# GLU output tiles in the score-row buffers, own buffers for the second half of w_out, and feed-forward products written ahead of the last tile's transposes

## The chip, the cores and the metric

One core of a Trainium2 chip runs one inference step of a hybrid encoder layer. The metric is the device time of one execution in microseconds (us).

## What is computed

The layer takes 2048 prompt frames and 64 sample frames of width 1024. All matrix products are in float32 accuracy: each operand is split into a high and a low part, and three products (high by high, high by low, low by high) are summed. Cut to what matters here:

```
hm   = rmsnorm(x) * (1 + scale) + shift
proj = hm @ w_in                      # q, k, v of 8 heads, forget logits, u of the S5 groups
att  = softmax(q k^T / 8 + F_t - F_s) @ v, causal     # F: running sum of log sigmoid(gate)
z    = gelu(S5 scan of u)
ssm  = z * sigmoid(z @ w_glu)                         # the GLU
mix  = concat(att, ssm)
x    = x + g1 * rmsnorm(mix @ w_out)
hf   = rmsnorm(x) * (1 + scale2) + shift2
f    = (silu(hf @ w_gate) * (hf @ w_up)) @ w_down
x    = x + g2 * rmsnorm(f)
```

## The kernel before, in words

The stages follow one another: input projections and S5 scan (to about 696 us), the GLU and then attention head by head (to about 1275 us), the output projection tile by tile (to about 1480 us), the gate and up products of the feed-forward layer (to about 2407 us), and the down product. The text of the program says what depends on what; the framework then sets the order of the instructions on each engine by a schedule of its own, so that a piece that is written early may stand late and the reverse. Every engine takes its own instructions strictly in that order. Loads and stores are issued by the queues of SP (nearly all) and ACT (the GLU's outputs) and by POOL. The transfers of SP and ACT share eight completion counters, dealt out in turn in one common order: an issue that takes a counter waits until the transfer eight places ahead in that order has landed.

**GLU** (`glu`, L914 to L958). `ZS` holds z in DRAM. For each of 4 column blocks b, four tiles `zr` (or `row1` buffers, for odd b) are loaded from `ZS`, split into `zh` and `zl`, and for each of 4 output row blocks o two halves are computed: 12 products into a PSUM bank (L945 to L947), a tanh on ACT (L949) into the tile `mo`, and a product with z on DVE (L953). When both halves of a tile are done, ACT issues its store to `MIXS` (L951), behind the first tanh of the next tile. `mo` is one of two buffers named "raw"; these two also serve the cached keys and values of the sample heads (L1086) and the second half of w_out (L1197).

**Attention** (`scores` L982, `values` L1043). For each head h and each block qb of 512 frames, SP loads `qs`, `kk`, `fb` and `vv` (L994 to L998). The scores of 128 frames fill one row buffer: four `row0` buffers for even qb, four `row1` buffers for odd. ACT takes the exponential (L1029). `values` transposes the rows on PE (L122), ACT copies them out of PSUM (`ph`, `pf`: L1067, L1064), and PE multiplies by `vv` (L1071, L1072). The GLU's end and the loads of head 0 overlap.

**Second half of w_out** (`wo_half`, L964). Four pieces of 128 by 1024 are loaded into "raw" (L970); ACT copies each into its high part `woh` (L974), POOL subtracts into the low part `wol` (L975). A "raw" buffer is free again when POOL is done.

**mix0** (`mix_half`, L1164) prepares the first tile of the output projection from `MIXS`: a load, a scaling on POOL (L1172), a subtraction on DVE (L1179), into buffers `mr`, `mh`, `ml` of its own.

**Turn to the feed-forward layer** (L1382 to L1408). Tile t=16 (the 64 sample rows) is the last of the output projection. Its two sums in PSUM go through two norms (L1263 to L1280), the transposes to `hf` (L122), a store to `HB`, and combinations `bh`, `bl` of column blocks (L1321). The gate and up products are formed from seven combinations of blocks (index i) for two matrices; L1449 is the matmul. The first three weight tiles are split ahead of time (`pre`). `weight_sums` forms the combinations of weights on POOL at tile 12.

Of the kernel before, what the change touches and what calls it, by code (L numbers as in the profile page):

```python
# [9 lines left out]
F32 = mybir.dt.float32  # L10
# [9 lines left out]
D = 1024  # L20
KD = 8
NP = 2048
# [46 lines left out]
def hybrid_layer(ctx: ExitStack, tc: tile.TileContext, I, O):  # L69
# [844 lines left out]
    def glu():  # L914
        def load(b, j):
            if b % 2 == 0:
                z = gw.tile([128, L, GC], F32, name="zr", bufs=4)
            else:
                z = at.tile([128, NP], F32, name="row1", bufs=4)[:, :L * GC].rearrange("p (s c) -> p s c", s=L)
            sp.dma_start(z, ZS[j * 128:(j + 1) * 128, :, b * GC:(b + 1) * GC])  # L920
            return z

        nb = CH // GC
        zr = [[load(0, j) for j in range(4)], [load(1, j) for j in range(4)]]
        out = None
        for b in range(nb):
            zz = []
            for hf in range(2):
                for j in range(4):
                    zh = gw.tile([128, 4, GC], F32R, name="zh", bufs=8)  # L930
                    zl = gw.tile([128, 4, GC], F32R, name="zl", bufs=8)
                    split(zh, zl, zr[b][j][:, 4 * hf:4 * hf + 4])
                    zz.append((zh, zl))
            if b + 2 < nb:
                zr.append([])
            for o in range(4):
                os_ = slice(o * 128, (o + 1) * 128)
                mo = raws[-1].tile([128, 2, 512], F32, name="raw", bufs=2)
                mo = mo.rearrange("p a b -> p (a b)")[:, :L * GC]
                mv = mo.rearrange("p (c s) -> p s c", s=L)  # L940
                for hf in range(2):
                    ps = bank("pt")[:, :4 * GC]
                    for k in range(4):
                        zh, zl = zz[4 * hf + k]
                        pe.matmul(ps, glu_h[:, k, os_], zh, start=k == 0, stop=False)  # L945
                        pe.matmul(ps, glu_h[:, k, os_], zl, start=False, stop=False)
                        pe.matmul(ps, glu_l[:, k, os_], zh, start=False, stop=k == 3)  # L947
                    s = slice(4 * hf, 4 * hf + 4)
                    act.activation(mv[:, s], ps.rearrange("p (s c) -> p s c", c=GC), AF.Tanh, scale=0.25)  # L949
                    if hf == 0 and out is not None:  # L950
                        act.dma_start(*out)  # L951
                        out = None
                    dve.scalar_tensor_tensor(mv[:, s], mv[:, s], 1.0, zr[b][o][:, s], op0=OP.add, op1=OP.mult)  # L953
                    yield
                out = (MIXS[os_, b * L * GC:(b + 1) * L * GC], mo)
                if b + 2 < nb:
                    zr[b + 2].append(load(b + 2, o))
        act.dma_start(*out)  # L958
# [4 lines left out]
    def wo_half(pool_, half, raw_of, lo_eng):  # L963
        h_ = pool_.tile([128, 4, D], F32R, name=f"woh{half}")  # L964
        l_ = pool_.tile([128, 4, D], F32R, name=f"wol{half}")
        for k in range(4):
            wo[4 * half + k] = h_[:, k], l_[:, k]
        for k in range(4):
            raw = raw_of()
            sp.dma_start(raw, w_out[:, 4 * half + k, :])  # L970
            if half:
                yield
                yield
            act.activation(h_[:, k], raw, AF.Copy)  # L974
            lo_eng.tensor_sub(l_[:, k], raw, f32(h_[:, k]))  # L975
            yield
# [184 lines left out]
        for _ in xs:  # L1161
            pass

    def mix_half(mp, t, half, bufs):  # L1164
        r = 128 if t < 16 else 64
        b, q = (t // 4, t % 4 * 128) if t < 16 else (3, 512)
        src = MIX[b][:, q:q + r] if half == 0 else MIXS[:, t * 128:t * 128 + r]
        s = 0.25 if half else 1.0
        mr = mp.tile([128, 4, 128], F32, name="mr", bufs=min(bufs, MR))
        sp.dma_start(mr[:, :, :r], src.rearrange("(k p) t -> p k t", p=128))  # L1170
        th_ = mp.tile([128, 4, 128], F32R, name="mh", bufs=bufs)
        pool.tensor_scalar(th_[:, :, :r], mr[:, :, :r], s, 0.0, op0=OP.mult, op1=OP.add)  # L1172
        if t == 16:
            tl_ = None
            dst = th_[:, :, 64:128]
        else:
            tl_ = mp.tile([128, 4, 128], F32R, name="ml", bufs=bufs)
            dst = tl_
        dve.scalar_tensor_tensor(dst, mr[:, :, :r], s, f32(th_[:, :, :r]), op0=OP.mult, op1=OP.subtract)  # L1179
        return th_, tl_  # L1180
# [6 lines left out]
    for h in range(H):  # L1187
        st = {"k": [], "v": [], "f": [], "l": {}}
        if h == 1:
            gl_.close()  # L1190
            wop = ctx.enter_context(ExitStack())
            wop2 = wop.enter_context(tc.tile_pool(name="wout2", bufs=1, side="right", reuse_waits="tile"))
        if h:
            side.append(sample_head(h - 1))
        if h == 2:
            side.append(wo_half(wop2, 1, lambda: raws[-1].tile([128, 2, 512], F32, name="raw", bufs=2).rearrange(
                "p a b -> p (a b)"), pool))  # L1197
        if h == H - 1:
            side.append(sample_head(h))
        for qb in range(4):  # L1200
            rows = []
            interleave(scores(h, qb, st, rows), pend, 4 * (qb + 1), n_pend)
            pend, n_pend = values(h, qb, st, rows), 4 * qb + 4
    mix0 = mix_half(wop2, OT[0], 1, 1)
    for g in (*side, pend):
        for _ in g:
            pass
# [122 lines left out]
        return raws_  # L1330

    def weight_sums(fp, raws_):
        src = []
        for m, raw in enumerate(raws_):
            ss = g8_tile()
            s = ss.rearrange("p (i k f) -> p i k f", i=4, k=4)
            x11, x12 = raw[:, 0:4, 0:128], raw[:, 4:8, 0:128]
            x21, x22 = raw[:, 0:4, 128:256], raw[:, 4:8, 128:256]
            sums4(pool, x11, x12, x21, x22, [s[:, i] for i in range(4)])
            pool.dma_start(WST[m][fp].rearrange("p i k -> p (i k)"), ss)  # L1340
            src.append((x11, s[:, 1], x12, s[:, 2], s[:, 0], x22, s[:, 3]))
        return src

    def down_sums(j):
        raw = g8_tile().rearrange("p (a n) -> p a n", a=2)
# [37 lines left out]
    for i, t in enumerate(OT):  # L1383
        if i + 1 < len(OT):
            t2 = OT[i + 1]
            if i >= 2:
                parts[t2, 1] = mix_half(mp, t2, 1, 3)
            parts[t2, 0] = mix_half(mp, t2, 0, 3)
        if i >= 3:
            accs[t] = [bank("mm") for _ in range(2)]  # L1390
            out_half(t, 1, parts.pop((t, 1)), accs[t])
        out_half(t, 0, parts.pop((t, 0)), accs[t])
        if late:
            out_turn(*late)
            combine_for(late[0])
        if i in (9, 11):
            prep(0, (i - 9) // 2, dve, g8)
        if i == 12:
            raws_ = raw_weights(g8, 0)
            src_w = weight_sums(0, raws_)  # L1400
        if i == len(OT) - 1:
            for n_ in range(3):
                pre.append(rsplit(wring[0], [128, 4, 128], src_w[n_ % 2][n_ // 2], ("wh", "wl")))
        late = t, out_norm(t, accs.pop(t))
    out_turn(*late)
    combine_for(late[0])
    p3.close()
# [18 lines left out]
    def ffn_pair(u, fp, after, src_w):  # L1426
# [7 lines left out]
        for i, role in enumerate("ababcbc"):  # L1434
            bh, bl = (b[:, :, :n] for b in blk[i])
            for m in range(2):
                if pre:
                    wh, wl = pre.pop(0)
                else:
                    turn_w[0] += 1  # L1440
                    v = src_w[m][i] if u == 0 else weight(i, m, fp)
                    wh, wl = rsplit(wring[turn_w[0] % 2], [128, 4, 128], v, ("wh", "wl"))
                first = (role, m) not in banks
                if first:
                    banks[role, m] = bank("up")[:, :n]
                acc = banks[role, m]
                for k in range(4):
                    for q, (w, x) in enumerate(((wh, bh), (wh, bl), (wl, bh))):
                        pe.matmul(acc, w[:, k, :], x[:, k], start=first and k == 0 and q == 0,  # L1449
                                  stop=k == 3 and q == 2, skip_group_check=True)  # L1450
# [40 lines left out]
    for u in range(3):  # L1491
        for fp in range(NF // 2):
# [17 lines left out]
            def after(i):  # L1510
                if nxt:
                    prep(nxt, i, (dve, pool)[i % 2], g8)
                if u == 0 and i == 2 and fp + 1 < NF // 2:
                    nxt_w.extend(weight_sums(fp + 1, raws_))
                if u == 0 and i == 5 and fp + 2 < NF // 2:
                    raws_[:] = raw_weights(g8b, fp + 2)

# [144 lines left out]
```

## Time and profile before

| | us |
|---|---|
| three runs | 2883.9 median (2878.4 to 2885.53) |
| the profiled execution | 2882.82 |
| its span in the trace | 2881.0 |
| PE busy | 2658.4 (92%) |
| DVE busy | 2011.6 (70%) |
| ACT busy | 1410.5 (49%) |
| POOL busy | 1309.0 (45%) |

The mean granted TensorE clock of the profiled execution was 0.959 of full speed. The span is the time from the first to the last instruction of the trace; 1.8 us of the execution lie around it. Busy shares are means over all stages. In the strip of 40 slices of 72 us PE stands at 8 or 9 tenths nearly everywhere behind the first quarter; slices 10 to 13 (from 648 us) read 9, 6, 9 and 7, which are the GLU's stretch and that of the second half of w_out, and slice 21, which holds the turn to the feed-forward layer (about 1480 us), reads 7.

### The profile page before, as it was taken

What the parts mean: (1) busy time and instruction counts of PE and PEld (TensorE: products, weight loads), DVE (VectorE), ACT (ScalarE), POOL (GpSimd) and SP (SyncE); (2) the same over time, 40 slices, a digit from 0 to 9 for tenths busy, and PEclk for the clock granted to TensorE, in tenths of its full rate; (3) what the DMA queues carried; (4) which work ended last, traced back from release to release, by engine and by line L of the source; (5) the groups of instructions that cost most, each with busy time, mean ns of one, the idle gap of its engine ahead of it and who ended that gap; (6) DMA issues with size and microseconds to landing.
All of it is one profiled execution on the core that took longest, in us unless ns stands there. A gap on an engine that the chain in (4) does not pass through costs nothing.

```text
span 2881.0 us, 43890 instructions
## 1 busy us (share of the span) xinstructions
PE 2658.4 (92%) x14580; PEld 2297.8 (80%) x14580; DVE 2011.6 (70%) x3591; ACT 1410.5 (49%) x2724; POOL 1309.0 (45%) x1643
## 2 busy tenths in 40 slices
PE   6699988889697999999978999999999999999997
PEld 2478866667575887778768999999998999888775
DVE  4966567654385887755659988996689886567556
ACT  2343454543276887855553333434354544444333
POOL 3673789892144444433527876663247432001002
PEclk8899989989798999999989999999999999999999
DMA  8565766768644344227855554895569777668554
GB/s 249 162 206 113 175 171 173 193 173 230 157 111 107 101 123 125 78 89 228 268 175 197 204 196 186 301 312 173 177 200 322 236 220 239 195 189 300 172 167 154
DMA packets 470499, 543.48 MB, mean 189 GB/s; under 512 B 112560, under 2 KB 322192, under 8 KB 467456
## 3 DMA queue, kind: packets, MB, share of 16 engines
q1 hardware_dynamic: 445616, 454.72, 54.4%
q0 software_dynamic: 22352, 81.63, 7.6%
q10 hardware_dynamic: 2304, 4.33, 0.4%
q8 instruction: 115, 1.88, 0.3%
q14 instruction: 112, 0.92, 0.1%
HBM read 369.29 MB, written 167.07 MB: 186 GB/s over the span
## 4 chain that ended last, share of the span: by engine, by line
PE 65%; POOL 10%; DVE 9%; DMA 7%; issue 5%; ACT 3%; SPq 1%; DVEq 0%; ACTq 0%; POOLq 0%
PE bank L1449 26%; PE bank L122 5%; PE bank L1578 4%; PE bank L1579 4%; PE bank L1577 4%; PE bank L438 4%; PE bank L1072 2%; PE bank L1071 2%; PE bank L1242 2%; PE bank L1243 2%; PE bank L1017 2%; PE bank L1245 2%; PE bank L1018 2%; DVE wl L1368 2%; POOL cm L703 1%
## 5 line engine op out<-in xcount | busy, mean ns | idle before, releaser
L1449 PE MATMUL bank<-bh,wh 128*128 128x384 f32 (+1 forms) x1848 | 597.5, 324 | 23.7 <-DVE u L1462 7.7
L1449 PE MATMUL bank<-bh,wl 128*128 128x384 f32 (+1 forms) x1848 | 595.4, 322 | 0.0
L1449 PE MATMUL bank<-bl,wh 128*128 128x384 f32 (+1 forms) x1848 | 595.3, 322 | 0.0
L1449 PEld LDWEIGHTS bank<-bh,wh 128*128 128x128 f32 x1848 | 349.2, 189 | 29.7 <-issue 13.5
L1449 PEld LDWEIGHTS bank<-bl,wh 128*128 128x128 f32 x1848 | 349.0, 189 | 0.0
L1449 PEld LDWEIGHTS bank<-bh,wl 128*128 128x128 f32 x1848 | 348.9, 189 | 0.0
L1367 ACT ACTIVATE wh<-wv 128x512 fp32r<-128x512 f32 x308 | 193.7, 632 | 268.6 <-PE bank L1449 211.8
L1368 DVE TENSOR_TENSOR wl<-wv,wh 128x512 fp32r<-128x512 f32 x308 | 286.5, 934 | 46.4 <-ACT wh L1367 40.3
L1485 POOL DMA_DIRECT2D HS<-hx x231 | 126.7, 550 | 275.4 <-DVE hx L1478 269.7
L144 POOL TENSOR_SCALAR var<-ss 128x1 f32<-128x1 f32 (+2 forms) x69 | 28.5, 414 | 481.1 <-ACT sq L1615 220.3
L1578 PE MATMUL bank<-wl,hh 128*128 128x512 f32 x608 | 236.3, 390 | 0.0
L1577 PE MATMUL bank<-wh,hh 128*128 128x512 f32 x608 | 235.5, 389 | 0.0
L1579 PE MATMUL bank<-wh,hl 128*128 128x512 f32 x608 | 235.5, 390 | 0.0
L122 PE MATMUL bank<-ident,row 128*128 128x128 f32 (+1 forms) x1120 | 174.9, 275 | 25.6 <-ACT pf L1064 18.4
L1029 ACT ACTIVATE row<-row,mx 128x1024 f32<-128x1024 f32 (+2 forms) x192 | 171.6, 899 | 37.1 <-DMA kk<-KHL 19.0
L1368 DVE TENSOR_TENSOR wl<-g,wh 128x512 fp32r<-128x512 f32 x154 | 171.2, 1119 | 21.7 <-ACT wh L1367 21.4
L122 PEld LDWEIGHTS bank<-ident,row 128*128 128x128 f32 (+1 forms) x1120 | 134.0, 142 | 56.1 <-ACT pf L1064 22.2
L1564 DVE TENSOR_TENSOR wl<-wr,wh 128x512 fp32r<-128x512 f32 x152 | 105.9, 696 | 93.7 <-ACT wh L1563 93.5
L1563 ACT ACTIVATE wh<-wr 128x512 fp32r<-128x512 f32 x152 | 95.0, 625 | 134.7 <-PE bank L1581 117.2
L1570 DVE TENSOR_TENSOR hl<-hr,hh 128x512 fp32r<-128x512 f32 x152 | 105.6, 695 | 74.9 <-ACT hh L1569 74.9
L1367 ACT ACTIVATE wh<-g 128x512 fp32r<-128x512 f32 x154 | 94.6, 629 | 127.7 <-PE bank L1449 100.1
L1022 DVE CUSTOM_DVE_ANT_0 row<-bank,fb,mx 128x512 f32<-128x512 f32 (+2 forms) x192 | 124.0, 646 | 37.0 <-PE bank L1018 23.8
(449 smaller groups left out, 7020.5 us busy)
## 6 DMA issues: line engine op xcount, KB each, us to landing
wv<-WST SPq DMA_DIRECT2D x176, 256.0 KB
HS<-hx POOLq DMA_DIRECT2D x154, 192.0 KB, 4.5
raw<-in_w_in SPq DMA_DIRECT2D x52, 512.0 KB
raw<-in_w_ada SPq DMA_DIRECT2D x48, 512.0 KB
WST<-g POOLq DMA_DIRECT2D x22, 1024.0 KB, 4.4
wr<-WDT SPq DMA_DIRECT2D x88, 256.0 KB
hr<-HS SPq DMA_DIRECT2D x77, 272.0 KB
hr<-HS SPq DMA_DIRECT2D x75, 256.0 KB
```

The costliest lines, as they stand in the source:

```text
L122: pe.transpose(out, in_, ident[:n, :n])
L438: pe.matmul(acc, w[:, k, :], x[k][:, c0:c0 + cn], start=k == 0 and q == 0, stop=k == KD - 1 and q == len(terms) - 1)
L1022: dve.tensor_tensor_reduce(out=row[:, c0:c0 + cn], in0=ps[:, :cn], in1=st["f"][c0 // 1024][:, c0 % 1024:c0 % 1024 + cn], scale=1.0, scalar ...
L1029: act.activation(row[:, c0:c0 + cn], row[:, c0:c0 + cn], AF.Exp, scale=-1.0, bias=mx, accum_out=l4[:, c0 // 1024, i:i + 1])
L1367: act.activation(hi, src, AF.Copy)
L1368: dve.tensor_sub(lo, src, f32(hi))
L1449: pe.matmul(acc, w[:, k, :], x[:, k], start=first and k == 0 and q == 0, stop=k == 3 and q == 2, skip_group_check=True)
L1485: pool.dma_start(HS[i][fp, :, c0:c0 + n], v)
L1564: dve.tensor_sub(wl, wr, f32(wh))
L1577: pe.matmul(acc, hh[:, s], wh, start=st, stop=False)
L1578: pe.matmul(acc, hh[:, s], wl, start=False, stop=False)
L1579: pe.matmul(acc, hl[:, s], wh, start=False, stop=en)
```

## The change

It has three parts. In the GLU the tiles `mo` of the first three column blocks and the first three row blocks take one of the four `row0` buffers; o = 3 and the last column block stay with "raw". The second half of w_out gets two buffers `wr` of its own, and mix0 uses the same two buffers after it, for its load and for its two results. At the feed-forward turn four weight tiles are split ahead, not three; the 48 matmuls that use them are written ahead of t=16's transposes, with a new order of PSUM banks; and the eight weight sums are spread over tiles 13 and 14 in the program's text.

```diff
@@ glu
-                mo = raws[-1].tile([128, 2, 512], F32, name="raw", bufs=2)
-                mo = mo.rearrange("p a b -> p (a b)")[:, :L * GC]
+                if b < nb - 1 and o < 3:
+                    mo = at.tile([128, NP - 512], F32, name="row0", bufs=4)[:, :L * GC]
+                else:
+                    mo = raws[-1].tile([128, 2, 512], F32, name="raw", bufs=2)
+                    mo = mo.rearrange("p a b -> p (a b)")[:, :L * GC]
...
         if h == 2:
-            side.append(wo_half(wop2, 1, lambda: raws[-1].tile([128, 2, 512], F32, name="raw", bufs=2).rearrange(
-                "p a b -> p (a b)"), pool))
+            side.append(wo_half(wop2, 1, lambda: wop2.tile([128, D], F32, name="wr", bufs=2), pool))
...
-    mix0 = mix_half(wop2, OT[0], 1, 1)
+    m_in = wop2.tile([128, D], F32, name="wr", bufs=2)
+    m_hl = wop2.tile([128, 2, 4, 128], F32R, name="wr", bufs=2)
+    mix0 = mix_half(None, OT[0], 1, 1, m_in[:, :512].rearrange("p (k t) -> p k t", k=4), m_hl[:, 0], m_hl[:, 1])
...
         if i == 12:
             raws_ = raw_weights(g8, 0)
-            src_w = weight_sums(0, raws_)
+            src_w, sgen = weight_sums(0, raws_)
+        if i in (13, 14):
+            next(sgen, None)
         if i == len(OT) - 1:
-            for n_ in range(3):
+            for n_ in range(4):
                 pre.append(rsplit(wring[0], [128, 4, 128], src_w[n_ % 2][n_ // 2], ("wh", "wl")))
         late = t, out_norm(t, accs.pop(t))
+    plan.update(up=(4, 5, 0, 1, 2, 3, 6, 7))
+    pre_acc = []
+    for n_, (wh, wl) in enumerate(pre):
+        bh, bl = blk[n_ // 2]
+        acc = bank("up")[:, :384]
+        pre_acc.append(acc)
+        for k in range(4):
+            for q, (w, x) in enumerate(((wh, bh), (wh, bl), (wl, bh))):
+                pe.matmul(acc, w[:, k, :], x[:, k], start=k == 0 and q == 0, stop=k == 3 and q == 2,
+                          skip_group_check=True)
     out_turn(*late)
     combine_for(late[0])
```

The order of the instructions changes at three places. The rows below are in the order in which the engine takes them; a name left of an arrow is written, one right of it read, and brackets name whom the instruction waits for (DMAHW0 to DMAHW7 are the eight shared completion counters).

ACT in the GLU, from the fifth output tile on, before (L949 is the tanh, L951 the store, L1029 the exponential of head 0's first scores):

```order
L949 ACTIVATE raw<-bank_6939 128x4x66 [waits DMAHW1_49,PE_49]
L949 ACTIVATE raw<-bank_6955 128x4x66 [waits PE_49]
L951 DMA MIXS<-raw 128x528 [waits DMAHW1_49,DVE_49]
L1029 ACTIVATE row_7244,l_7243<-row_7244,mx 128x128 [waits DVE_49]
L1029 ACTIVATE row_7301,l_7243<-row_7301,mx 128x256 [waits DVE_49]
L1029 ACTIVATE row_7324,l_7243<-row_7324,mx 128x384 [waits DVE_49]
L949 ACTIVATE raw<-bank_6973 128x4x66 [waits DMAHW6_49]
L949 ACTIVATE raw<-bank_6989 128x4x66 [waits PE_49]
L1029 ACTIVATE row_7349,l_7243<-row_7349,mx 128x512 [waits DVE_49]
L951 DMA MIXS<-raw 128x528 [waits DMAHW4_49,DVE_49]
L949 ACTIVATE raw<-bank_7007 128x4x66 [waits DMAHW1_49,PE_49]
```

The same tiles after (L952 is the tanh, L954 the store):

```order
L952 ACTIVATE row_6938<-bank_6939 128x4x66 [waits PE_49]
L952 ACTIVATE row_6972<-bank_6973 128x4x66 [waits DMAHW4_49,PE_49]
L952 ACTIVATE row_6938<-bank_6955 128x4x66 [waits PE_49]
L952 ACTIVATE row_6972<-bank_6989 128x4x66 [waits PE_49]
L952 ACTIVATE row_7006<-bank_7007 128x4x66 [waits DMAHW6_49,PE_49]
L954 DMA MIXS<-row_6938 128x528 [waits DMAHW4_49,DVE_49]
L954 DMA MIXS<-row_6972 128x528 [waits DMAHW6_49,DVE_49]
L952 ACTIVATE raw<-bank_7041 128x4x66 [waits PE_49]
L952 ACTIVATE row_7006<-bank_7023 128x4x66 [waits PE_49]
```

Up to three tiles are now in work at a time, and the exponentials of head 0 have gone behind the twelfth store of the GLU. The stores still wait for counters.

SP and the second half of w_out: before, the four loads stand among the loads of heads 2 and 3, far behind the GLU; after, they stand right behind the GLU's last tiles, among the loads of the sample heads and of heads 0 and 1. SP after (L973 is the w_out load):

```order
L973 DMA wr<-in_w_out 128x1024 [waits DMAHW5_49,DVE_49,PE_49]
L973 DMA wr<-in_w_out 128x1024 [waits DMAHW6_49]
L1092 DMA raw<-in_cache_k 128x4x64 [waits DMAHW4_49,DMAHW7_49,DMAHW2_49,DVE_49]
L1093 DMA raw<-in_cache_k 128x4x64 [waits DMAHW1_49]
L997 DMA qs<-QHL_60 128x1x512 [waits PE_49]
L1095 DMA raw<-in_cache_v 128x4x64 [waits DMAHW3_49]
L1092 DMA raw<-in_cache_k 128x4x64 [waits DMAHW0_49,DVE_49]
L1093 DMA raw<-in_cache_k 128x4x64 [waits DMAHW5_49]
L1095 DMA raw<-in_cache_v 128x4x64 [waits DMAHW6_49]
L973 DMA wr<-in_w_out 128x1024 [waits DMAHW7_49,Pool_49]
L973 DMA wr<-in_w_out 128x1024 [waits Pool_49]
L997 DMA qs<-QHL_60 128x1x512 [waits DMAHW1_49,PE_49]
```

The first pair waits for the GLU's last reads, the second for POOL to be done with the first; mix0's load stands right behind the last row, and the loads for head 1 behind that.

ACT's copies `woh` after (L977), now in head 0's first two blocks of values:

```order
L1032 ACTIVATE row_7486,l_7398<-row_7486,mx 128x896 [waits DVE_49,Pool_49]
L1055 ACTIVATE rb<-bank_7515 64x512 [waits PE_49]
L1070 ACTIVATE ph<-bank_7521 128x256 [waits PE_49]
L977 ACTIVATE woh_9339<-wr 128x1024 [waits DMAHW5_49,DMASW0_49]
L1070 ACTIVATE z3h<-bank_7538 128x128 [waits PE_49]
L1032 ACTIVATE row_7509,l_7398<-row_7509,mx 128x1024 [waits DVE_49,Pool_49]
L977 ACTIVATE woh_9339<-wr 128x1024 [waits DMAHW6_49]
```

The third and fourth `woh` follow 10 and 14 rows behind the second. Each waits at its place for its load, with the exponentials and copies of head 0 behind it.

PE at the turn to the feed-forward layer, before: the 48 first products stand ahead of t=16's transposes already. The last of them, the transposes (L122, 128x64) and the next products:

```order
L1449 MATMUL bank_16215<-bh_14138,wh 128x384
L1449 MATMUL bank_16215<-bl_14139,wh 128x384
L1449 MATMUL bank_16215<-bh_14138,wl 128x384
L122 MATMUL bank_16082<-ident,xt 128x64 [waits DVE_49,Activation_49]
L122 MATMUL bank_16082<-ident,xt 128x64 x3
L122 MATMUL bank_16091<-ident,xt 128x64 [waits Activation_49]
L122 MATMUL bank_16091<-ident,xt 128x64 x3
L1449 MATMUL bank_16166<-bh_16132,wh 128x384 [waits Activation_49]
```

After, where the first 24 of them (L1426) end and the other 24 begin, around the transposes of the tile before t=16 (128x128):

```order
L122 MATMUL bank_16004<-ident,xt 128x128 [waits DVE_49,Activation_49]
L122 MATMUL bank_16004<-ident,xt 128x128 x3
L122 MATMUL bank_16013<-ident,xt 128x128 [waits Activation_49]
L122 MATMUL bank_16013<-ident,xt 128x128 x3
L1426 MATMUL bank_16123<-bl_14138,wh 128x384
L1426 MATMUL bank_16123<-bh_14137,wl 128x384
L1426 MATMUL bank_16084<-bh_14135,wh 128x384 [waits DVE_49,PE_49]
L1426 MATMUL bank_16084<-bl_14136,wh 128x384
```

Ahead of the same transposes stand the same 48 products, but the last 24 of them now use the banks of t=16's own sums and wait until DVE has read those. The order of the weight sums on POOL at tiles 12 to 14 is what it was.

## Rows read from the trace of the kernel before

**Rows 1.** The page: the chain that ended last, by engine.

```profile
PE 65%; POOL 10%; DVE 9%; DMA 7%; issue 5%; ACT 3%; SPq 1%; DVEq 0%; ACTq 0%; POOLq 0%
```

**Rows 2.** PE's waits, 696 to 775 us: us in total, times, longest.

```profile
PE bank L945 <- ACT raw L949: 30.4, 5, 12.2
```

**Rows 3.** ACT's waits, 696 to 775 us.

```profile
ACT raw L949 <- DMA fb<-FP: 28.7, 3, 10.8
ACT row L1029 <- DMA kk<-KHL: 19.0, 1, 19.0
ACT raw L949 <- DMA MIXS<-raw: 8.1, 3, 4.7
```

**Rows 4.** The chain of work, 700 to 775 us: start, duration, what.

```profile
754.64 11.12 DMA fb<-FP
765.84 0.33 ACTq L951
```

**Rows 5.** Windows: length, busy (instructions) by engine, PEclk, DMA share, GB/s.

```profile
710.00:770.00 60.00, 28.17 (x146) 25.29 (x147) 14.11 (x32) 8.07 (x19) 6.53 (x13) 0.71 0.75 178
...
740.00:750.00 10.00, 3.71 (x17) 3.72 (x18) 2.57 (x6) 3.15 (x10) 2.10 (x4) 0.50 0.97 230
750.00:760.00 10.00, 4.87 (x22) 4.59 (x22) 3.65 (x7) 1.12 (x2) 2.16 (x5) 0.67 1.00 206
```

**Rows 6.** Transfers, 696 to 775 us.

```profile
DMA packets 21182, 14.13 MB, mean 179 GB/s; under 512 B 13498, under 2 KB 16890, under 8 KB 21178
```

**Rows 7.** PE's waits, 855 to 930 us, then ACT's, 780 to 930 us.

```profile
PE bank L122 <- ACT pf L1064: 18.4, 3, 14.4
...
ACT woh L974 <- DMA raw<-in_w_out: 21.8, 3, 14.6
```

**Rows 8.** The chain of work, 855 to 930 us.

```profile
857.19 6.44 DMA raw<-in_w_out
...
868.41 8.62 DMA raw<-in_w_out
...
902.83 12.07 DMA raw<-in_w_out
```

**Rows 9.** Windows of 10 us behind the fourth load of w_out.

```profile
900.00:910.00 10.00, 3.14 (x20) 2.42 (x18) 0.64 (x2) 0.30 (x1) 2.04 (x3) 0.77 0.53 135
910.00:920.00 10.00, 2.51 (x12) 2.51 (x13) 1.89 (x3) 3.01 (x5) 3.92 (x3) 0.50 0.09 30
920.00:930.00 10.00, 10.00 (x58) 8.50 (x56) 6.92 (x21) 6.60 (x14) 4.47 (x6) 0.88 0.29 78
```

**Rows 10.** L974 and L975: duration ns min/median/max, first and last start.

```profile
L974 ACT ACTIVATE woh<-raw x4: 1052/1057/1066, 863.7 to 914.9; 128x1024 fp32r<-128x1024 f32 x4
...
L975 POOL TENSOR_TENSOR wol<-raw,woh x4: 2356/2376/2404, 864.9 to 916.1; 128x1024 fp32r<-128x1024 f32 x4
```

**Rows 11.** ACT's groups, 795 to 830 us: busy, mean ns, idle before.

```profile
L1029 ACT ACTIVATE row<-row,mx 128x1024 f32<-128x1024 f32 (+7 forms) x19 | 18.5, 983 | 4.9 <-DVE mx L1022 3.8 <-issue 1.1
L1067 ACT ACTIVATE ph<-bank 128x512 fp32r<-128x512 f32 (+2 forms) x15 | 7.5, 534 | 1.7 <-PE bank L122 1.7
```

**Rows 12.** The window of head 0's values, 795 to 830 us.

```profile
795.00:830.00 35.00, 34.97 (x213) 27.91 (x212) 31.08 (x93) 29.16 (x65) 13.17 (x14) 1.00 0.30 76
```

**Rows 13.** PE's timeline at the turn; in brackets the idle time before.

```profile
1495.11 1.09 PE L122 MATMUL bank<-ident,xt 64*128 64x64 f32 x8 [12.10 <-DVE xt L1280]
1501.17 1.01 PE L1449 MATMUL bank<-bh,wh 128*128 128x384 f32 x2 [4.98 <-ACT bh L1321]
```

**Rows 14.** L1449's first form, and DVE's reads of t=16's sums.

```profile
L1449 PE MATMUL bank<-bh,wh x1848: 290/334/686, 1473.6 to 2407.3; 128*128 128x384 f32 x124, 128*128 128x288 f32 x61
...
L1264 DVE TENSOR_TENSOR o<-bank,lo x2: 674/678/682, 1484.9 to 1486.9; 64x512 f32<-64x512 f32 x2
```

**Rows 15.** Windows: the first products behind the turn; the step to the down product.

```profile
1500.00:1510.00 10.00, 8.46 (x35) 7.96 (x36) 6.33 (x6) 6.05 (x6) 4.28 (x2) 0.69 0.65 150
...
2400.00:2410.00 10.00, 10.00 (x71) 9.59 (x70) 6.65 (x14) 4.10 (x9) 2.17 (x3) 1.00 0.99 342
```

More of the change, by code (lines that the diff above doesn't have):

```diff
@@ L1162, in interleave, with mix_half @@
             pass
-    def mix_half(mp, t, half, bufs):
+    def mix_half(mp, t, half, bufs, mr=None, th_=None, tl_=None):
         r = 128 if t < 16 else 64
@@ L1168, in mix_half @@
         s = 0.25 if half else 1.0
-        mr = mp.tile([128, 4, 128], F32, name="mr", bufs=min(bufs, MR))
+        if mp:
+            mr = mp.tile([128, 4, 128], F32, name="mr", bufs=min(bufs, MR))
+            th_ = mp.tile([128, 4, 128], F32R, name="mh", bufs=bufs)
         sp.dma_start(mr[:, :, :r], src.rearrange("(k p) t -> p k t", p=128))
-        th_ = mp.tile([128, 4, 128], F32R, name="mh", bufs=bufs)
         pool.tensor_scalar(th_[:, :, :r], mr[:, :, :r], s, 0.0, op0=OP.mult, op1=OP.add)
@@ L1176, in mix_half @@
         else:
-            tl_ = mp.tile([128, 4, 128], F32R, name="ml", bufs=bufs)
+            tl_ = tl_ if mp is None else mp.tile([128, 4, 128], F32R, name="ml", bufs=bufs)
             dst = tl_
@@ L1332, in weight_sums @@
     def weight_sums(fp, raws_):
-        src = []
+        src, work = [], []
         for m, raw in enumerate(raws_):
@@ L1338, in weight_sums, with run @@
             x21, x22 = raw[:, 0:4, 128:256], raw[:, 4:8, 128:256]
-            sums4(pool, x11, x12, x21, x22, [s[:, i] for i in range(4)])
-            pool.dma_start(WST[m][fp].rearrange("p i k -> p (i k)"), ss)
+            work.append((m, x11, x12, x21, x22, s, ss))
             src.append((x11, s[:, 1], x12, s[:, 2], s[:, 0], x22, s[:, 3]))
-        return src
+        def run():
+            for m, x11, x12, x21, x22, s, ss in work:
+                sums4(pool, x11, x12, x21, x22, [s[:, i] for i in range(4)])
+                pool.dma_start(WST[m][fp].rearrange("p i k -> p (i k)"), ss)
+                yield
+        return src, run()
     def down_sums(j):
@@ L1436, in ffn_pair @@
             for m in range(2):
-                if pre:
-                    wh, wl = pre.pop(0)
-                else:
+                ready = pre_acc.pop(0) if pre_acc else None
+                if ready is None:
                     turn_w[0] += 1
@@ L1444, in ffn_pair @@
                 if first:
-                    banks[role, m] = bank("up")[:, :n]
+                    banks[role, m] = bank("up")[:, :n] if ready is None else ready
                 acc = banks[role, m]
-                for k in range(4):
+                for k in range(4 if ready is None else 0):
                     for q, (w, x) in enumerate(((wh, bh), (wh, bl), (wl, bh))):
@@ L1513, in after @@
                 if u == 0 and i == 2 and fp + 1 < NF // 2:
-                    nxt_w.extend(weight_sums(fp + 1, raws_))
+                    new, run = weight_sums(fp + 1, raws_)
+                    nxt_w.extend(new)
+                    for _ in run:
+                        pass
                 if u == 0 and i == 5 and fp + 2 < NF // 2:
```

## The prediction

> **What bounds the kernel now.** I read the page's chain first [rows 1]: 65% of the span is PE, 7% DMA, 5% issue. So PE is the bound in most stages, and a change that leaves PE's work as it is can only win where PE stands still, or where it runs at a lower clock because it stood still. PE's waits and windows of 10 us show three such stretches that the change touches.
>
> In the GLU PE waits 30.4 us, in 5 pieces, for the tanh on ACT [rows 2]. The window from 710 to 770 us holds 28.17 us of PE work in 60 us at a mean granted clock of 0.71, and 0.50 in the 10 us from 740 [rows 5]. The reader should look at what ACT itself waits for there [rows 3]: only 8.1 us of the tanh's waits end with a store to `MIXS`, which frees a "raw" buffer. 28.7 us end with a load of head 0's `fb`, which the tanh does not read, and once ACT stands 19.0 us for a `kk`. The chain says how [rows 4]: `fb` lands at 765.8, then ACT's queue passes L951, the store, and then the tanh runs. A store that waits for a shared counter holds ACT.
>
> Near w_out PE waits 18.4 us for copies that stand behind `woh` on ACT, and ACT waits 21.8 us for the loads [rows 7], which take 6.44, 8.62 and 12.07 us on the chain [rows 8]. Behind the last one the clock is 0.77, 0.50 and 0.88 [rows 9].
>
> At the turn to the feed-forward layer PE stands still for 12.10 and 4.98 us [rows 13].
>
> **GLU tiles.** Six buffers instead of two for most tiles: the same 32 tanhs, 16 stores and loads, so no work is added, only order. What there is to gain in all: 31.8 us of idle PE time in that window [rows 5], and by the granted clock another 28.17 x 0.29 = 8.2 us, 40.0 us together. Two things hold it down. The buffers proper are worth the 8.1 us of [rows 3]; the counters stay. And the transfers: 14.13 MB move between 696 and 775 us at 179 GB/s on average [rows 6]. With the DMA engines busy for 0.97 and 1.00 of a window, 230 and 206 GB/s moved [rows 5]. At 230 GB/s the 14.13 MB take 61.4 us of the 79, at 206 they take 68.6: a gain of 17.6 or 10.4 us, if the same loads stay inside the stretch. I take 10 us, the busier window, near also to the 8.1 us of the buffers. The ends are 0 and 17.6 us; they grow to 40.0 only if loads of later blocks leave the stretch. The cover that is lost: head 0's first scores filled part of PE's stall in this stretch, and now stand behind tiles of the third column block, since they need `row0` buffers whose stores have landed. I price that at nothing, since GLU products run in that time in their place.
>
> A rule speaks against this part. Of 21182 packets here 13498 are under 512 bytes [rows 6], and a fully busy window moves 206 to 230 GB/s, while at 2400 us a share of 0.99 moves 342 [rows 5, 15]. The Trainium skill (DMA: Bandwidth & Descriptors, Specifications) puts the least transfer for line rate at 512 bytes, since smaller ones are done as a read, a change and a write back. The rows agree as far as the rate goes. By that rule small pieces, not buffers, set this stretch, and the term would be near 0; that case is a rival below.
>
> **Second half of w_out.** Removed: the 18.4 us of PE waits and, by the clock of [rows 9], 3.14 x 0.23 + 2.51 x 0.50 + 10.0 x 0.12 = 3.2 us, together 21.6. Added: the same four loads, copies of 1.06 us and subtractions of 2.36 us [rows 10] right behind the GLU, while head 0's first values run. PE is 34.97 of 35 us busy there and ACT 29.16 [rows 12], so a wait on ACT reaches PE soon. The first pair of loads is issued together. Behind the GLU's last store stand one exponential, `rb` and `ph` ahead of the first `woh`: 0.98 + 0.53 [rows 11] and about 0.6, 2.1 us. Of a landing time of 6.44 us 4.3 show. The second pair goes out when POOL is done with the first, 2.36 us behind the copy, and takes 8.62 us, 11 us in all. Between the first and the third `woh` ACT has five exponentials of 0.98, three `ph` of 0.53, a `woh` of 1.06, and three shorter copies, estimated at 0.5 each from the `ph`: 9.1 us, so 1.9 show. Together 6.2 us come back, and 15 are won. The ends: nothing shows (21.6 won), or both pairs show with the longest landing, 2 x 12.07 = 24.1 (2.5 us lost). I stay with the shorter landings because few transfers ran at this time, a DMA share of 0.30 at 76 GB/s [rows 12]. The four copies, 4.2 us of ACT, move from one place to another and count as nothing: ACT has 5.8 us left in the window, and the 9.5 us of POOL fit in its 21.8. Behind the second pair SP holds a `qs` and the `kk` of head 1, which are needed a whole head later. mix0's load, its POOL and DVE steps stand behind the second pair too; DVE's step stands in the middle of head 0's last scores, so if the pair is late DVE is held as well.
>
> **The turn to the feed-forward layer.** The order shows that the 48 matmuls stood ahead of t=16's transposes already. So nothing new fills the 12.10 us. What changes is where 24 of them run. 48 matmuls and 8 transposes took from 1473.6 [rows 14] to 1483.0 (1495.11 less 12.10, [rows 13]), about 0.2 us each. The first 24 now end near 1478; the others wait until DVE has read the two sums, 1485.6 and 1487.6 [rows 14], and need 4.7 us at the full clock or 9.4 at half of it, so they end between 1490 and 1495, just ahead of the transposes at 1495.11, which come from the norms and do not move. For: PE is busy until shortly before the next products, which ran at a clock of 0.69 for 8.46 us [rows 15], so up to 2.6 us could be won. Against: at half clock the last of them may push the transposes by some 2 us. I take 1 us won; ends 2.6 won and 2 lost. The fourth split, the banks and the generator of weight sums cost nothing: POOL's order is the same, and the fourth split was issued a little later before. At the step to the down product PE is busy 10.00 of 10 us [rows 15]; its splits come in another order among themselves, and I leave it at 0.
>
> **Sum.** 10 + 15 + 1 = 26 us against the profiled execution's 2882.8 gives 2856.8. The median of the runs is 1.1 us above the profiled execution, so 2858 is the forecast.
>
> **The rivals.**
>
> *Both stretches open up.* The loads of later blocks leave the GLU, and w_out's are hidden: 2883.9 - 40.0 - 21.6 = 2822; with 17.6 in the GLU, 2845. For it: the DMA engines are idle for a quarter of the stretch, a share of 0.75 [rows 5]. Against: the counters that hold ACT stay. Chance 0.15.
>
> *Transfers bound the GLU.* The stores and loads in small pieces take the time they took, and ACT waits at other stores instead. Only w_out counts: 2868. For it: shares of 0.97 and 1.00 at 206 to 230 GB/s. Against: the mean share of 0.75 over the stretch. Chance 0.15.
>
> *The waits only change places.* The GLU's is the transfers', and w_out's loads show again near 800 us for about as long as they did: 2883.9 with a few us to either side. Likewise the feed-forward part does not do what it says, as the order shows. Chance 0.15.
>
> *Slower.* ACT in order behind w_out. The loads go out while the last stores and the sample heads' loads are under way; each of the four lands as the slowest did and none is covered: 4 x 12.07 = 48.3 us against the 21.6 removed. With the GLU between 0 and 10 us that is 2901 to 2911. It decides from the point where the waits for w_out near 800 us exceed 21.6 us and the GLU's gain together. For it: PE has no slack there [rows 12]. Against: two loads at a time go out together, and few other transfers run [rows 12]. Chance 0.08.
>
> The forecast has the rest, 0.47, with its own range of 2843 to 2875.
>
> **How the numbers follow.** About 0.3%, 8.7 us, is what a measurement of this kernel can tell from no change, so faster means below 2875 and slower above 2893. Faster: 0.46 of the forecast, 0.15, and 0.13 of the second rival, 0.74. Same: 0.13 of the third rival and 0.03 of the others, 0.16. Slower: 0.08 and 0.02 of the third, 0.10. The range from 2834 to 2886 leaves out the fast half of the first rival, the slow end of the third and the slower case, under 0.2 together.
>
> **What would show it.** In the GLU, the wait of PE for the tanh should fall from 30.4 us to about 20, the DMA share rise and the attention's first full window come about 10 us earlier. ACT's wait for w_out should fall from 21.8 to under 10 us and stand between 780 and 830; the windows that were at 900 to 930 should show a clock of 1.00. The wait of 12.10 us should be split into one of about 8 ahead of the 24 matmuls and a short one behind them, with the transposes as long behind the tile's norms as now. The forecast is wrong if the tanh's waits for counters stay at 28.7 us, or if `woh` waits over 20 us at its new place.

## The result, and the profile after

The change takes 2847.8 us (median of 4 runs, 2846.8 to 2850.7) against 2882.8 before (4 runs): a ratio of 0.988, interval [0.986, 0.990], 35.0 us less. The forecast was 2858 with a range of 2834 to 2886, so the time lies inside and 10 us below the forecast. The profiled execution has a span of 2845.5 us, 35.5 less than before.

Where it went is read from the first and last instruction of the lines that open and close a stage. The profile of the change, first products of the GLU and of the values:

```profile
L948 PE MATMUL bank<-zh,glu_h x128: 278/286/589, 697.2 to 780.7; 128*128 128x264 f32 x128
...
L1074 PE MATMUL bank<-ph,vv x288: 278/395/628, 784.6 to 1240.7; 128*128 128x512 f32 x112, 128*128 128x256 f32 x16, 128*128 128x384 f32 x16
```

The same of before:

```profile
L945 PE MATMUL bank<-zh,glu_h x128: 280/286/589, 696.1 to 789.5; 128*128 128x264 f32 x128
...
L1071 PE MATMUL bank<-ph,vv x288: 278/396/628, 793.3 to 1270.5; 128*128 128x512 f32 x112, 128*128 128x256 f32 x16, 128*128 128x384 f32 x16
```

The last value product is one of another form, `z3h`, and starts at 1241.0 us with the change and at 1270.7 us before. The table has one profiled execution per column, in us; the experiments of the next section stand beside the change. Each stage ends where the next one begins: attention is from the first to the last value product, the "turn" from t=16's last product to the first product behind its transposes.

| stage | before | change | change, again | part 1 alone | part 2 alone | part 3 alone |
|---|---|---|---|---|---|---|
| GLU to first value product | 97.2 | 87.4 | 89.5 | 89.2 | 94.0 | 93.9 |
| attention | 477.4 | 456.4 | 453.1 | 474.3 | 454.8 | 478.6 |
| output projection | 202.7 | 201.6 | 203.0 | 201.3 | 201.9 | 202.3 |
| turn | 27.8 | 27.9 | 28.4 | 27.8 | 28.0 | 29.0 |
| gate and up products | 906.4 | 901.8 | 898.3 | 904.2 | 901.6 | 914.3 |
| down product | 473.4 | 473.2 | 474.5 | 473.2 | 474.5 | 473.2 |
| median of all runs | 2882.8 | 2847.8 | 2850.2 | 2872.3 | 2858.7 | 2886.0 |

So the GLU gave 9.8 us in the profiled execution, attention 21.0, the gate and up products 4.6, the output projection 1.1, the turn nothing; the GLU began 1.1 us later than before. What PE waits for, 690 to 900 us of the change, to be held against [rows 2, 7]:

```profile
PE bank L948 <- ACT raw L952: 18.2, 3, 13.8
PE bank L948 <- ACT row L952: 5.6, 2, 4.9
PE bank L122 <- ACT pf L1067: 4.4, 1, 4.4
```

The tanh costs PE 23.8 us where it cost 30.4, and `pf` behind w_out 4.4 where it cost 18.4. ACT's own waits in the same stretch, to be held against [rows 3, 7]:

```profile
ACT raw L952 <- DMA vv<-VHL: 19.9, 2, 17.2
...
ACT raw L952 <- DMA fb<-FP: 7.7, 1, 7.7
...
ACT row L952 <- DMA vm<-VHL: 5.9, 1, 5.9
...
ACT woh L977 <- DMA wr<-in_w_out: 4.8, 1, 4.8
```

No tanh waits for a store to free its tile any more (8.1 us before). But 33.5 us of its waits end with loads that it does not read, where 28.7 did. Before, ACT also stood 19.0 us for a `kk` in front of an exponential that does not read it either [rows 3]; no such wait is left. Counted alike, ACT's waits for loads that the waiting instruction does not read fell from 47.7 to 33.5 us. The wait for w_out is a single one of 4.8 us, and the chain of work shows its place:

```profile
795.15 5.74 DMA wr<-in_w_out
...
800.91 1.06 ACT woh L977
```

Windows of the change: the GLU's 60 us (as far behind its start as [rows 5]), the new wait, and one of those that [rows 9] had:

```profile
711.10:771.10 60.00, 34.88 (x226) 32.57 (x225) 20.15 (x42) 10.53 (x20) 10.35 (x21) 0.77 0.79 200
...
800.00:810.00 10.00, 5.77 (x19) 4.66 (x20) 5.26 (x17) 9.09 (x19) 7.19 (x5) 0.66 0.34 118
...
900.00:910.00 10.00, 9.83 (x69) 7.43 (x68) 7.53 (x24) 8.82 (x21) 3.43 (x5) 1.00 0.44 110
```

In the GLU 6.7 us more of PE's work fall into the same 60 us, and the transfers run at 200 GB/s instead of 178. The wait for w_out leaves a mark at 800 us, a clock of 0.66, and the windows at 900 us stand at 1.00. The turn, PE's timeline, to be held against [rows 13]:

```profile
1454.24 0.66 PE L1426 MATMUL bank<-bh,wh 128*128 128x384 f32 x1 [6.22 <-DVE o L1269]
...
1464.47 0.79 PE L122 MATMUL bank<-ident,xt 64*128 64x64 f32 x8 [4.03 <-DVE xt L1285]
1470.48 1.01 PE L1471 MATMUL bank<-bh,wh 128*128 128x384 f32 x2 [5.22 <-ACT bh L1326]
```

The 12.10 us have become 6.22 and 4.03, with 24 matmuls between them, and the wait behind is 5.22 instead of 4.98.

### The profile page after: what moved, and what is told of

It is laid out like the page before. It is cut to its first block, busy times and chain, and to the rows that moved or that the text cites. A ratio compares the mean times of both kernels' runs of the same rounds, so it can differ in the third digit from the quotient of the medians.

```text
span 2845.5 us, 43913 instructions
## 1 busy us (share of the span) xinstructions
PE 2644.9 (93%) x14580; PEld 2289.3 (80%) x14580; DVE 2011.1 (71%) x3591; ACT 1408.9 (50%) x2724; POOL 1303.3 (46%) x1643
## 4 chain that ended last, share of the span: by engine, by line
PE 67%; POOL 11%; DVE 8%; DMA 6%; issue 5%; ACT 3%; SPq 1%; DVEq 0%; ACTq 0%; POOLq 0%
PE bank L1471 26%; PE bank L122 5%; PE bank L1603 5%; PE bank L1604 5%; PE bank L1602 5%; PE bank L438 4%; PE bank L1075 2%; PE bank L1074 2%; PE bank L1020 2%; PE bank L1248 2%; PE bank L1247 2%; PE bank L1021 2%; PE bank L1250 2%; POOL cm L704 2%; POOL cm L702 2%
## 5 line engine op out<-in xcount | busy, mean ns | idle before, releaser
L1471 PE MATMUL bank<-bh,wh 128*128 128x384 f32 (+1 forms) x1832 | 590.3, 323 | 22.7 <-DVE u L1479 6.1
L1471 PE MATMUL bank<-bh,wl 128*128 128x384 f32 (+1 forms) x1832 | 588.7, 321 | 0.8 <-DVE wl L1379 0.8
L1471 PE MATMUL bank<-bl,wh 128*128 128x384 f32 (+1 forms) x1832 | 588.7, 321 | 0.0
L122 PE MATMUL bank<-ident,row 128*128 128x128 f32 (+1 forms) x1120 | 171.8, 273 | 12.7 <-DVE row L216 7.0
L1379 DVE TENSOR_TENSOR wl<-g,wh 128x512 fp32r<-128x512 f32 x154 | 161.6, 1057 | 21.9 <-ACT wh L1378 21.6
L122 PEld LDWEIGHTS bank<-ident,row 128*128 128x128 f32 (+1 forms) x1120 | 132.5, 141 | 41.6 <-issue 12.8
```

Of the source, the lines that this page charges most:

```text
L122: pe.transpose(out, in_, ident[:n, :n])
L1379: dve.tensor_sub(lo, src, f32(hi))
```

## The experiments

Each was timed against the kernel before on the same chip, whose median was 2883.1 us beside the three parts alone and the stores on POOL, 2886.0 beside the change without part 3 and the two kernels with z loads on POOL, and 2886.8 beside the last two. The theory: the three parts act each in its stretch, and in the GLU it is the shared counters and the buffers that hold ACT. The rivals: the transfers bound the GLU, or part of one gain belongs to another part.

### The parts one by one

Part 1 alone, the rest as before:

```diff
+                if b < nb - 1 and o < 3:
+                    mo = at.tile([128, NP - 512], F32, name="row0", bufs=4)[:, :L * GC]
+                else:
```

> The kernel before with the first part of the change alone (row0 buffers for the GLU tiles). Theory: the three parts act on stretches of their own, so from the start of the GLU to the first value product this kernel takes 87 to 88 us, as with the whole change, against 97.2 before, and the total is some 10 us less than before (about 2873); the wait for w_out near 900 us stays at 18 us on PE. Rival: the GLU got shorter only because the w_out loads and their buffers left the two raw buffers; then the stretch keeps its 97 us and the total stays within 3 us of before.

Measured: 2872.3 us, ratio 0.996 [0.995, 0.997], 10.9 less; the stretch took 89.2 us, 1 us more than expected. PE's waits, 696 to 930 us:

```profile
PE bank L122 <- ACT pf L1067: 20.3, 4, 14.9
PE bank L948 <- ACT raw L952: 18.2, 3, 13.6
PE bank L948 <- ACT row L952: 7.5, 2, 5.8
```

The GLU's waits are those of the whole change, and w_out's are those of before: the part works in its own stretch.

Part 2 alone:

```diff
-            side.append(wo_half(wop2, 1, lambda: raws[-1].tile([128, 2, 512], F32, name="raw", bufs=2).rearrange(
-                "p a b -> p (a b)"), pool))
+            side.append(wo_half(wop2, 1, lambda: wop2.tile([128, D], F32, name="wr", bufs=2), pool))
```

with mix0 in the `wr` buffers as in the change.

> The kernel before with the second part alone (own buffers wr for w_out and mix0). Theory: the attention stretch from the first value product to the last takes about 456 us against 477.2 before, the GLU stretch keeps its 97 us, and the total is about 21 us less than before (2862). Rival: part of the 21 us comes from the GLU part, since the loads of the heads come earlier when the GLU ends earlier; then the gain here is near 15 us, the PE waits and clock that the prediction counted, and the total is about 2868.

Measured: 2858.7 us, ratio 0.991 [0.990, 0.993], 24.4 less; attention took 454.8 us, the GLU 94.0. PE's waits, 696 to 930 us:

```profile
PE bank L945 <- ACT raw L949: 31.0, 5, 12.4
PE bank L122 <- ACT pf L1064: 1.5, 1, 1.5
```

The theory holds: the gain in attention, 22.6 us, is there without the GLU part, and larger than the 15 us that had been summed. The 94.0 us of the GLU, whose order is that of before, are scatter; part 3 alone shows 93.9.

Part 3 alone:

```diff
-            for n_ in range(3):
+            for n_ in range(4):
...
+    plan.update(up=(4, 5, 0, 1, 2, 3, 6, 7))
```

with the 48 matmuls and the generator as in the change.

> The kernel before with the third part alone (two products ahead, new bank order, sums as a generator). Theory: the 4 to 5 us that the whole change won behind the turn come from this part, because PE works until shortly before the next products and so has more clock and a shorter wait afterwards; the total is 4 to 5 us less than before (2878). Rival: it is worth nothing by itself, total within 1.5 us of before, and the 4 to 5 us come from somewhere upstream.

Measured: 2886.0 us over 12 runs, ratio 1.001 [1.000, 1.002]. The expected 4 to 5 us are not there; the rival, no gain within 1.5 us, comes nearer, though the kernel was 2.9 us longer. The turn took 29.0 us and the gate and up products 914.3 in the profiled execution, the longest of all columns. The same question from the other side, the whole change without part 3:

```diff
-            for n_ in range(4):
+            for n_ in range(3):
...
-    plan.update(up=(4, 5, 0, 1, 2, 3, 6, 7))
```

> The whole change without its third part (the turn to the feed-forward layer as before). Theory: the third part is worth nothing, since its 48 matmuls stood ahead of the transposes before as well, and the feed-forward stage's 901 to 914 us scatter from run to run; total within 4 us of the whole change (2848). Rival: the third part is worth 4 to 5 us when the rest of the change is there; total about 2852.

Measured: 2850.0 us, ratio 0.987 [0.986, 0.989], the same as the whole change within its interval; turn 27.9 us, gate and up products 901.8. Part 3 is worth nothing that can be measured, alone or with the others.

The totals add up: 10.9 + 24.4 - 2.9 = 32.4 us by single parts, 35.0 for the whole (36.6 in the second timing).

### What holds the GLU

The whole change with the stores on POOL's queue, which takes none of the eight counters:

```diff
-                        act.dma_start(*out)
+                        pool.dma_start(*out)
```

(and the same for the last store)

> The whole change, and the GLU's stores to MIXS issued by POOL instead of ACT, so that they take none of the eight counters that SP's loads share and ACT holds no store. Theory that the counters hold ACT: the tanh's waits that end with loads (33 us with the whole change) go, PE's 24 us of waits for the tanh in the GLU fall below 10, the stretch falls from 87 to about 70 us, and the total from 2848 to about 2830. Rival that the transfers bound the stretch: the waits move to PE waiting for zh and zl, the stretch stays within 3 us of 87 and the total within 3 us of 2848. A third: POOL, which splits z, is held by the stores and the stretch gets longer than 87 us.

Measured: 2845.9 us, ratio 0.987 [0.985, 0.989], the change's within its interval; the stretch took 82.6 us. No tanh waits for a load any more. PE's waits, 696 to 930 us:

```profile
PE bank L948 <- POOL zh L125: 19.3, 4, 9.2
```

and POOL's, 696 to 800 us:

```profile
POOL zh L125 <- DMA row<-ZS: 13.7, 5, 8.3
POOL zh L125 <- DMA zr<-ZS: 11.0, 2, 9.4
```

So the theory and its first rival were both half right. The counters did hold ACT for 33.5 us and all of that went; but the z loads, which stand behind head 0's loads on SP, were next and cost PE 19.3 us.

The whole change with the later z loads on POOL, the stores left on ACT:

```diff
-            sp.dma_start(z, ZS[j * 128:(j + 1) * 128, :, b * GC:(b + 1) * GC])
+            (pool if b >= 2 else sp).dma_start(z, ZS[j * 128:(j + 1) * 128, :, b * GC:(b + 1) * GC])
```

> The whole change, with the z loads of the third and fourth column block issued by POOL, so that they stand behind no load of head 0 on SP and take none of the shared counters; the stores stay on ACT. Theory that order and counters set the stretch: PE's waits in the GLU (24 us with the whole change) fall to about 15, the stretch from 87 to about 78 us, total about 2838. Rival that the transfer engines set it: the 15.2 MB of the stretch take their time in any order, the stretch stays within 3 us of 87 and the total within 3 us of 2848.

Measured: 2856.0 us, ratio 0.989 [0.987, 0.991], which overlaps the change's; the stretch took 93.8 us, longer than with the change (87.4 to 89.5), which neither theory had said. ACT's waits, 696 to 800 us:

```profile
ACT raw L952 <- DMA vv<-VHL: 19.0, 1, 19.0
...
ACT row L952 <- DMA kk<-KHL: 14.3, 1, 14.3
...
ACT raw L952 <- DMA kk<-KHL: 3.7, 1, 3.7
```

and PE's, 696 to 830 us:

```profile
PE bank L948 <- ACT raw L952: 14.7, 1, 14.7
PE bank L948 <- POOL zh L125: 6.7, 2, 3.5
PE bank L948 <- ACT row L952: 5.3, 1, 5.3
PE bank L949 <- DVE zl L126: 2.5, 1, 2.5
```

With the z loads out of the common order, the stores of ACT stand among head 0's loads alone, and three tanhs wait 37.0 us for loads that they do not read: the counters hold ACT as before. In PE's waits that is not what made the stretch longer, though: the tanh costs PE 20.0 us, less than with the change (23.8). What is new are 6.7 us for `zh` and 2.5 for `zl`, where the change had 1.4 for `zl`. POOL issues the later z loads in its own order, and two of these issues stand 13.9 and 18.7 us, until DVE comes to the instruction that they wait for.

Both on POOL:

> Stores and later z loads of the GLU both issued by POOL. Order and counters: with the stores alone on POOL PE waited 19.3 us for zh, and zh for z loads that stood behind head 0's on SP; those go too, the stretch falls from 83 to about 70 us, total about 2832. Transfer engines: stretch within 3 us of 83, total within 3 us of 2846. A third, POOL itself: its splits of z stand in order behind 24 issues of stores and loads, and stores behind products of DVE, so that PE waits for zh longer than 19 us and the stretch is over 87 us.

Measured: 2836.7 us, ratio 0.983 [0.982, 0.985]: faster than the change (the intervals do not meet) and the fastest kernel here. The stretch took 75.0 us. PE's waits, 696 to 800 us:

```profile
PE bank L1020 <- DMA kk<-KHL: 8.0, 1, 8.0
...
PE bank L948 <- POOL zh L125: 2.1, 3, 1.1
```

The window of [rows 5] in this kernel:

```profile
710.00:770.00 60.00, 45.77 (x327) 41.90 (x325) 31.19 (x64) 18.53 (x35) 21.73 (x41) 0.91 0.83 230
```

Its transfers, 699 to 769 us:

```profile
DMA packets 13299, 15.63 MB, mean 223 GB/s; under 512 B 5384, under 2 KB 8776, under 8 KB 13293
```

The same of the change, 697 to 777 us:

```profile
DMA packets 21752, 15.22 MB, mean 190 GB/s; under 512 B 13560, under 2 KB 16952, under 8 KB 21747
```

PE waits for the tanh no longer in its GLU products, and the longest wait is for head 0's keys. As many megabytes as moved in 80 us with the change moved in 70 us. The amount of data did not bound the GLU at 87 us. But 8176 packets fewer are under 512 bytes; what that means is taken up with the rivals below.

The last with all GLU tiles in the two "raw" buffers:

```diff
-                if b < nb - 1 and o < 3:
-                    mo = at.tile([128, NP - 512], F32, name="row0", bufs=4)[:, :L * GC]
```

> The kernel with the GLU's stores and later z loads on POOL, without the row0 buffers: all GLU tiles in the two raw buffers as before the change, w_out and the turn as changed. Theory that the counters alone held the GLU: two buffers are enough once ACT holds no store, the stretch stays near 75 us and the total near 2837. Rival that the buffers matter by themselves: with two of them each tanh waits for the store of two tiles before, and a store took 7 us from issue to landing on POOL's queue with row0 buffers; 14 such waits, partly covered, bring the stretch to 90 us or more and the total to 2850 or more.

Measured: 2854.8 us, ratio 0.990 [0.988, 0.991]; the stretch took 89.4 us. ACT's waits, 696 to 800 us:

```profile
ACT raw L949 <- DMA MIXS<-raw: 24.1, 7, 6.7
```

The buffers matter by themselves, as the rival said: with the counters gone, 24.1 us of the tanh's waits end with stores that free a tile. Six buffers and no counters are worth 14.4 us over two buffers and no counters. The whole stretch, with six buffers and with two:

```profile
697.50:772.50 75.00, 60.12 (x435) 55.03 (x433) 38.87 (x77) 26.46 (x50) 26.92 (x48) 0.93 0.81 221
...
699.60:789.00 89.40, 67.57 (x434) 61.98 (x433) 38.27 (x77) 25.92 (x49) 27.82 (x50) 0.83 0.70 187
```

Of the 14.4 us, 6.9 are idle time of PE, and 7.5 come from the same products running longer, at a granted clock of 0.83 instead of 0.93.

The whole change once more:

> The whole change again, on the same chip as the run beside it. Both theories: 2848 within 4 us, GLU stretch 87 to 89 us.

Measured: 2850.2 us, ratio 0.988 [0.986, 0.990]; stretch 89.5 us, half a us above what was expected.

## Why the prediction was right, and where its sizes were off

**GLU, 10 us.** Near in size, in part by luck: 9.8 us in the profiled execution, 10.9 us in total for the part alone. The stretch scatters: three executions of the old order took 97.2, 94.0 and 93.9 us, four of the new one 87.4 to 89.5, so by those means (95.0 and 88.8) the stretch itself gave 6 us; where the rest of the 10.9 comes from no run shows. Of the two reasons given for the cap one fell: the transfers are no bound at 87 us, since the same megabytes moved in a stretch of 75, and in one of 82.6 with as many small packets. The 10 us had been read from that reason, so that they came near is in part luck. The other, the counters, stands. One sign that was set fell too: "the forecast is wrong if the tanh's waits for counters stay at 28.7 us". They rose to 33.5 and PE still gained. The sign was set on too small a sum: it left out the 19.0 us that ACT stood before an exponential. With them, ACT's waits for unread loads fell by 14.2 us, and its 8.1 us of waits for stores went. What counts is PE's wait for the tanh, which fell by 6.6 us; it was 30.1 to 31.0 us in the three executions of the old order and 23.8 to 25.7 in the four of the new one. How much of that came from more tiles being in work and how much from the exponentials having moved is not shown.

**Second half of w_out, 15 us.** Right in mechanism and in place, too small in size: attention lost 21.0 us with the change and 22.6 with the part alone. Two terms were mis-sized. What was to come back, 6.2 us, came to 1.5 us of PE's waits in the part alone and 4.4 in the change: the first pair of loads, put at 4.3 us, showed not at all, since SP issued it at 781.2 us, ahead of the GLU's last store at 784.6; and the second pair, put at 1.9, showed 4.8 on ACT. It was to go out when POOL was done with the first piece, near 790.5 us; SP stood at the loads for the sample heads until 795.1. And what was removed was summed from w_out's waits and three windows alone. The whole stretch of attention says more:

```profile
793.30:1270.70 477.40, 450.56 (x2814) 364.89 (x2815) 355.54 (x1002) 369.59 (x808) 212.86 (x226) 0.98 0.39 99
```

before, and with part 2 alone

```profile
792.70:1247.50 454.80, 447.55 (x2815) 363.21 (x2815) 355.93 (x1002) 369.58 (x808) 214.05 (x227) 1.00 0.40 103
```

PE's idle time fell from 26.8 to 7.3 us, 19.6 less, 16.9 of which is the wait for `pf` near w_out (18.4 to 1.5); and the same 2814 matmuls took 3.0 us less at a clock of 1.00 instead of 0.98. The rest, near 3 us, are small waits that no term had counted.

**The turn, 1 us.** Nothing was won, as the order had let expect: 27.8 us before, 27.9 after. The wait split in two as forecast, into 6.22 and 4.03 us where about 8 and a short one had been said, and the transposes stood 21.9 us behind t=16's last product, 21.7 before. The step that failed was the clock: the busy stretch ahead of the transposes was to give back up to 2.6 us, but the 5.22 us of waiting for `bh` come behind it in any case. The first 10 us of products behind the turn, before and with the change, stand at 0.75 and 0.76:

```profile
1501.20:1511.20 10.00, 9.63 (x42) 9.13 (x43) 7.00 (x3) 5.05 (x5) 5.48 (x2) 0.75 0.68 184
...
1470.50:1480.50 10.00, 9.64 (x43) 9.13 (x44) 6.56 (x3) 5.58 (x6) 5.02 (x2) 0.76 0.68 183
```

**Gate and up products.** No term had the 4.6 us that they gave in the profiled execution. They came with part 2 (901.6 and 901.8 us without part 3) and not with part 3. In part 2 alone PE and SP have the order of before in this stage; on ACT, DVE and POOL a few neighbours change places (a `wh` and a `bh`, a `c` and a `wl`). Kernels without part 2 took 904.2 to 914.3 us, all those with it 898.3 to 905.2, so the two groups touch. Whether the swaps or the scatter of the stage made the 4.6 us stays open; no run tells them apart.

**The rivals.** "Both stretches open up" came half: the loads of w_out are nearly hidden, but the counters held ACT in the GLU, as had been said against it; the kernel with both on POOL, 2836.7 us, lies between its figures of 2822 and 2845. "Slower" did not come: two loads went out together and ACT waited 4.8 us, not 48. "The waits only change places" and "transfers bound the GLU" are refuted by the runs, the latter as the buffers and the queues moved the stretch between 75 and 94 us with the same bytes. The rule cited for it from the Trainium skill (DMA: Bandwidth & Descriptors, Specifications) was read too far in the prediction: small pieces may move below line rate, but here they were not what ended last. The fastest kernel also moves the stretch's data with fewer packets under 512 bytes (5384, where the change has 13560). Two other kernels hold these apart, the stores alone on POOL (699 to 779 us) and the z loads alone on POOL (702 to 797 us):

```profile
DMA packets 21008, 15.51 MB, mean 194 GB/s; under 512 B 13578, under 2 KB 16970, under 8 KB 21002
...
DMA packets 14520, 16.37 MB, mean 172 GB/s; under 512 B 5410, under 2 KB 8802, under 8 KB 14515
```

With all the small packets left the stretch fell to 82.6 us, and with 8150 fewer it took 93.8; with the two "raw" buffers, on the queues of the fastest kernel, it took 89.4. Fewer small packets alone did not shorten it. Whether they have a part in the last step, from 82.6 to 75.0 us, is left open.

## What to carry to other kernels

A wait that ends with a load which the instruction does not read is a sign of queueing: look for a transfer issued on the same engine, and see which counter or earlier transfer it stands behind. A store issued by a compute engine in the middle of its work can hold that engine for as long as unrelated loads take, here 17.2 us in one piece; a queue with counters of its own, and enough output buffers, have to come together before the full gain is there (75 us, against 82.6 to 93.8 with one of them missing or half done). A large load that blocks one in-order engine in a busy stage can cost less with buffers of its own and at an earlier place: the loads of w_out cost PE 18.4 us before and 1.5 to 4.4 so. Which of the two did it was not tried apart.

## What had not been expected of the hardware

With eight z loads (pieces of 66 values) on POOL's queue instead of SP's the packets under 512 bytes in the stretch fell from 13560 to 5410, about 1000 for each load. On POOL's queue they were no small packets: its row in the transfers of the kernel with the z loads alone there, 702 to 797 us (queue, packets, MB, share), has 3.4 KB per packet:

```profile
q0 software_dynamic: 640, 2.16, 9.9%
```

And the same order of instructions gave stretches that differ by 3 us in the GLU and by more in the gate and up products from one execution to the next, while the totals of a kernel agreed within 0.1 to 0.5%; a stage's gain of a few us cannot be read from one profile.
